# Layer norm in a four-layer decoder step: additions in place of reductions, and the variance products moved in TensorE's order

## The chip, the cores and the metric

The kernel runs on one core of a Trainium2 chip, as one program with one launch. The metric is the device time of a run in microseconds. The views come from one profiled execution of the program.

## The reference

One inference step of a decoder trunk with model width 1024 and four layers, for a prompt of 512 tokens and 8 sample tokens. Each layer has a token mixer (NSA attention, gMLP, HGRN2, NSA again) and then a SwiGLU FFN, and behind each of the eight stands a layer norm:

```python
def layer_norm(x, g, b):
    xf = x.astype(jnp.float32)
    mu = jnp.mean(xf, axis=-1, keepdims=True)
    var = jnp.mean(jnp.square(xf - mu), axis=-1, keepdims=True)
    return (xf - mu) * lax.rsqrt(var + LN_EPS) * g + b

def deepnorm(x, h, g, b):
    return layer_norm(DEEPNORM_ALPHA * x + h, g, b)
```

A ninth layer norm stands inside the gMLP mixer, on its gate values v. All of it is in float32.

## The kernel before

**Layout.** Activations lie transposed: features on the 128 partitions in eight blocks, the 520 tokens along the free axis. All work on tokens is done in two halves, columns 0 to 255 and 256 to 519. The norm takes two feature blocks at a time as one piece, so a half has four pieces j = 0 to 3, each 128 x 512 (first half) or 128 x 528 (second half).

**Products.** `mm` (L238 on) makes one output block of one half: for each k of 7 or 8 input blocks three products, high weight with high activation (L249), low weight with high activation (L250), high weight with low activation (L251). `Weights.need` at the start of an `mm` converts the weights of a unit ahead: two casts on ScalarE for the high parts (L101), two subtractions for the low parts (L102, mostly VectorE). Weight loads are issued on SP's queue, further ahead.

**Order.** The program is written out by hand: each engine's queue holds its instructions in the order in which Python emits them, and an engine works its queue in that order. Side work is written as generators. `mm` calls `tick()` after every second k, and each tick advances every generator in the list `par` by one `yield`. A tick is thus a place in TensorE's order, not a time. When an `mm` asks for activations of a half whose generator is not done, the rest of it is emitted at once (`Split.get`).

**The norm.** `ln` (L264) is such a generator, spawned when the last output block of a half has been added to x, and the sum over blocks (`add_sum`, L361 and L363, on GpSimd, the last on VectorE) is complete. In order:

- three waits (WM), then the product of the sums with a matrix of 1/1024 (L278), which gives the mean on all partitions;
- per piece a subtraction of the mean on VectorE (L285) and a square on ScalarE (L286), two pieces per tick; the squares of two pieces lie in one buffer;
- two reductions on VectorE (L294), each over the four blocks of one buffer, one per tick;
- WV = 0 waits, then two products with the same matrix (L299), accumulated: the variance;
- in the next tick the guess of the inverse root on ScalarE (`guess`: a table load at L333 if needed, logarithm L340, exponential L342); in the next one Newton step on VectorE (L349 to L353);
- per piece, one per tick: a multiply on VectorE (L307), then for each of its two blocks gain and bias on ScalarE into the high part (L312) and on GpSimd into x in place (L316); the low part, x minus high part, follows on VectorE (L272) one tick later.

There are 18 norm halves. In the second half of the last norm (`direct`) the eight blocks of squares go to the products without a reduction.

**What stands beside it.** A first half's norm runs beside the second half of the same output projection: seven blocks of four ticks, eight in the first NSA layer, or seven of three ticks (21 products) behind an FFN. A second half's norm runs beside the next stage, which computes its first blocks for the first half only: three hidden units of an FFN (two `mm` of four ticks each), or six blocks elsewhere; so in either case 24 ticks, and then TensorE needs the second half. The next stage's evictions stand among the norm's instructions: in an FFN after each eight ticks a SiLU on ScalarE (L419, with its own table, L333), a multiply on VectorE (L420), a cast on ScalarE (L210) and a subtraction on VectorE (L211); in gMLP a GELU after each four ticks, in HGRN2 a copy or a sigmoid, in NSA a copy or a sigmoid. The projections' evictions are L382 and L384 on VectorE. In gMLP the norm of v is followed by transposes (L479), copied on ScalarE (L482).

Of the kernel before, what the change touches and what calls it, by code (L numbers as in the profile page):

```python
# [11 lines left out]
OP = mybir.AluOpType  # L12
AX = mybir.AxisListType
# [7 lines left out]
CH = (8, 7, 7)  # L21
NFF = sum(CH)
SLOTS = 38
WM, WV = 3, 0


HORD, HF, HW, BUILD, SW0, SWAIT, HRATE, EARLY = (0, 1, 2, 3), 6, 1, 3, 0, 8, 2, 6
# [27 lines left out]
def wait(n):  # L55
    for _ in range(n):
        yield
# [60 lines left out]
class Split:  # L118
# [6 lines left out]
    def pair(self, j):  # L125
        if j not in self.h:
            self.h[j], self.l[j] = self.net.slot(FR), self.net.slot(FR)
        return self.h[j], self.l[j]
# [16 lines left out]
class Net:  # L145
# [118 lines left out]
    def ln(self, cols, li, sums, pair, X=None, out=None, direct=False):  # L264


        nc = self.nc
        late = []

        def rest():  # L270
            l, x, h = late.pop(0)
            nc.vector.tensor_sub(l, x, h.bitcast(FT))  # L272

        c0, c1 = cols
        n = c1 - c0
        yield from wait(WM)
        pm = self.ps()
        nc.tensor.matmul(pm[:, :n], self.ones, sums[:, :n], start=True, stop=True)  # L278
        yield
        q, sq = [], []  # L280
        for j in range(4):
            xs = pair(j, c0, c1)
            if j % 2 == 0:
                sq.append(self.flat()[:, :4 * n].rearrange("p (b t) -> p b t", b=4))
            nc.vector.tensor_sub(xs, xs, pm[:, None, :n].to_broadcast([128, 2, n]))  # L285
            nc.scalar.activation(sq[-1][:, 2 * (j % 2):2 * (j % 2) + 2], xs, AF.Square)  # L286
            if j % 2:
                yield
        for j in range(2):
            if direct:  # L290
                q += [sq[j][:, i] for i in range(4)]
            else:
                q.append(self.row()[:, :n])
                nc.vector.tensor_reduce(q[-1], sq[j].rearrange("p b t -> p t b"), op=OP.add, axis=AX.X)  # L294
            yield
        yield from wait(WV)
        pv = self.ps()
        for i, r in enumerate(q):
            nc.tensor.matmul(pv[:, :n], self.ones, r, start=i == 0, stop=i == len(q) - 1)  # L299
        y = self.row()[:, :n]  # L300
        yield
        self.guess([y], [pv[:, :n]])
        yield
        self.newton([y], [pv[:, :n]])
        for j in range(4):
            xs = pair(j, c0, c1)
            nc.vector.tensor_mul(xs, xs, y[:, None, :].to_broadcast([128, 2, n]))  # L307
            hl = X.pair(j) if X is not None else None
            for k in (0, 1):
                g, b = (t[:, li, 2 * j + k:2 * j + k + 1] for t in (self.gn, self.gb[:, :, 1]))  # L310
                if X is not None:
                    nc.scalar.activation(hl[0][:, k, c0:c1], xs[:, k], AF.Identity, scale=g, bias=b)  # L312
                if X is None and k == 0:
                    nc.scalar.activation(xs[:, k], xs[:, k], AF.Identity, scale=g, bias=b)
                else:
                    nc.gpsimd.tensor_scalar(xs[:, k], xs[:, k], g, b, op0=OP.mult, op1=OP.add)  # L316
            if X is not None:
                late.append((hl[1][:, :, c0:c1], xs, hl[0][:, :, c0:c1]))
            elif out is not None:
                out(j, c0, c1, xs)  # L320
            if len(late) > 1:
                rest()
            yield
        while late:
            rest()
            yield
# [1075 lines left out]
```

## Time and profile before

| | us |
|---|---|
| median of three runs | 3082.68 |
| lowest and highest | 3077.68, 3083.25 |
| the profiled execution | 3078.4 |
| its span, first to last instruction | 3076.7 |

The mean granted TensorE clock is 0.976 of full speed. In the rows below PE is TensorE, DVE VectorE, ACT ScalarE and POOL GpSimd. A line of the timeline gives start and duration in us, engine, source line, operation, output and input tile, shapes, the number of instructions merged into it, and in brackets how long the engine had been idle before and what released it. One matrix product in float32 stands there as two instructions.

### The profile page before, as it was taken

To read this page: it belongs to the slowest core of one execution; us is meant where nothing else is said; L and a number is where in the kernel's file an instruction comes from. 1 tells how busy PE (TensorE), PEld (TensorE's weight loads), DVE (VectorE), ACT (ScalarE), POOL (GpSimd) and SP (SyncE) were. 2 spreads that over 40 slices of the span, in tenths; PEclk is the share of its full clock that TensorE was granted. 3 is DMA by queue.
4 is the path that set the end of the run, shared out by engine and by line. 5 is a ranking of instruction groups with operands and counts; after the bars stand their busy time and mean duration, and the time that the engine had idled before them with its cause. 6 is when DMAs were issued, how large, how long until landed. Compare 5 with 4: busy or idle time off the path is not lost. (4 is left out here: it accounts for less than half of the span.)

```text
span 3076.7 us, 56298 instructions
## 1 busy us (share of the span) xinstructions
PE 2886.1 (94%) x22730; PEld 2759.4 (90%) x22730; DVE 1725.9 (56%) x3821; ACT 1293.8 (42%) x2902; POOL 473.4 (15%) x446
## 2 busy tenths in 40 slices
PE   8889889999989999999999999999988998899997
PEld 8888569999989899998899889999888876799997
DVE  4888655333566633337677773333668876533334
ACT  4666534222355432234445543122456665432322
POOL 0222141000031200004222230000312222400002
PEclk9999999999999999999999999999999999999999
DMA  5212532223223222322222223223222244233221
GB/s 173 69 59 80 165 124 90 96 77 108 71 83 97 76 90 92 101 89 71 78 71 73 76 100 94 94 80 95 81 87 63 63 155 130 97 97 94 85 86 40
DMA packets 136039, 280.61 MB, mean 91 GB/s; under 512 B 13026, under 2 KB 76002, under 8 KB 135778
## 3 DMA queue, kind: packets, MB, share of 16 engines
q1 hardware_dynamic: 127168, 261.86, 26.8%
q10 hardware_dynamic: 7458, 10.95, 1.0%
q0 software_dynamic: 1152, 4.19, 0.5%
q8 instruction: 179, 2.93, 0.4%
q14 instruction: 82, 0.67, 0.1%
HBM read 263.69 MB, written 13.27 MB: 90 GB/s over the span
## 5 line engine op out<-in xcount | busy, mean ns | idle before, releaser
L249 PE MATMUL ps<-g 128*128 128x256 f32 (+1 forms) x6176 | 1784.8, 289 | 19.5 <-ACT g L101 12.9
L250 PE MATMUL ps<-g 128*128 128x256 f32 (+1 forms) x6176 | 1758.0, 285 | 10.9 <-DVE g L102 5.8
L251 PE MATMUL ps<-g 128*128 128x256 f32 (+1 forms) x6176 | 1759.1, 285 | 3.0 <-DVE g L211 1.7
L249 PEld LDWEIGHTS ps<-g 128*128 128x128 f32 x6176 | 1180.2, 191 | 34.6 <-ACT g L101 13.3
L250 PEld LDWEIGHTS ps<-g 128*128 128x128 f32 x6176 | 1179.7, 191 | 18.3 <-DVE g L102 7.1
L251 PEld LDWEIGHTS ps<-g 128*128 128x128 f32 x6176 | 1177.5, 191 | 4.6 <-DVE g L211 2.6
L102 DVE TENSOR_TENSOR g<-g 128x512 fp32r<-128x512 f32 (+1 forms) x708 | 467.6, 711 | 59.9 <-ACT g L101 52.5
L101 ACT CAST g<-g 128x512 fp32r<-128x512 f32 (+1 forms) x788 | 426.6, 608 | 105.4 <-DVE g L102 98.1
L420 DVE TENSOR_TENSOR row<-row,ps 128x256 f32<-128x256 f32 (+1 forms) x176 | 74.8, 425 | 515.8 <-PE ps L251 515.8
L210 ACT CAST g<-row 128x256 fp32r<-128x256 f32 (+1 forms) x192 | 78.6, 410 | 503.4 <-DVE row L420 491.7
L361 POOL TENSOR_TENSOR row<-x 128x256 f32<-128x256 f32 (+1 forms) x16 | 13.3, 834 | 1452.1 <-DVE x L384 1003.1
L419 ACT ACTIVATE row<-ps 128x256 f32<-128x256 f32 (+1 forms) x176 | 67.6, 384 | 334.3 <-PE ps L251 334.1
L952 ACT ACTIVATE g<-g,nst 128x128 f32<-128x128 f32 (+3 forms) x256 | 143.0, 559 | 128.0 <-DVE nst L950 123.9
L999 PE MATMUL ps<-g 128*128 128x512 f32 x384 | 142.1, 452 | 1.2 <-DVE g L987 0.9
L964 POOL TENSOR_SCALAR g<-g,nst 128x128 f32<-128x128 f32 (+3 forms) x64 | 76.4, 1193 | 414.8 <-DVE nst L957 345.4
L950 DVE CUSTOM_DVE_ANT_0 g<-ps,ncst 128x128 f32<-128x128 f32 (+3 forms) x256 | 119.3, 485 | 37.2 <-PE ps L948 27.8
L382 DVE SCALAR_TENSOR_TENSOR x<-x,ps 128x256 f32<-128x256 f32 (+1 forms) x128 | 52.9, 422 | 153.3 <-PE ps L251 153.1
L948 PE MATMUL ps<-g 128*128 128x256 f32 (+2 forms) x512 | 124.2, 346 | 13.9 <-DVE kcS L830 5.4
L102 POOL TENSOR_TENSOR g<-g 128x512 fp32r<-128x512 f32 x80 | 105.7, 1342 | 162.4 <-ACT g L101 147.6
L384 DVE TENSOR_TENSOR x<-x,ps 128x256 f32<-128x256 f32 (+1 forms) x128 | 53.8, 424 | 135.7 <-PE ps L251 135.6
L211 DVE TENSOR_TENSOR g<-row,g 128x256 fp32r<-128x256 f32 (+1 forms) x192 | 81.7, 429 | 83.8 <-ACT g L210 83.8
L316 POOL TENSOR_SCALAR x<-x,lngn,lngb 128x256 f32<-128x256 f32 (+1 forms) x120 | 104.8, 886 | 144.7 <-ACT g L312 129.9
(239 smaller groups left out, 2842.2 us busy)
## 6 DMA issues: line engine op xcount, KB each, us to landing
g<-ffn_in SPq DMA_DIRECT2D x176, 512.0 KB, 3.6
g<-ffn_out SPq DMA_DIRECT2D x64, 448.0 KB, 3.3
g<-nsa_in SPq DMA_DIRECT2D x42, 512.0 KB, 3.8
cm<-cache_cmp SPq DMA_DIRECT2D x64, 256.0 KB, 3.6
g<-cache_slc SPq DMA_DIRECT2D x128, 128.0 KB, 2.7
g<-cache_win SPq DMA_DIRECT2D x32, 512.0 KB, 5.4
g<-ffn_out SPq DMA_DIRECT2D x32, 512.0 KB, 3.5
g<-hgrn_in SPq DMA_DIRECT2D x32, 512.0 KB, 4.0
```

The costliest lines, as they stand in the source:

```text
L101: self.nc.scalar.copy(h[:, a:b], r[:, a:b])
L102: (self.sub[a > 0] or self.nc.vector).tensor_sub(l[:, a:b], r[:, a:b], h[:, a:b].bitcast(FT))
L210: self.nc.scalar.copy(h, src)
L211: self.nc.vector.tensor_sub(l, src, h.bitcast(FT))
L249: nc.tensor.matmul(p[:, :n], H[:, s], a, start=k == 0, stop=False)
L250: nc.tensor.matmul(p[:, :n], L[:, s], a, start=False, stop=False)
L251: nc.tensor.matmul(p[:, :n], H[:, s], b, start=False, stop=k == nk - 1)
L316: nc.gpsimd.tensor_scalar(xs[:, k], xs[:, k], g, b, op0=OP.mult, op1=OP.add)
L948: nc.tensor.matmul(p[:, :nn], q, kt[:, s, :nn], start=s == 0, stop=s == 1)
L950: nc.vector.tensor_tensor_reduce(P, p[:, :n], tri[:, 512 - n:], 1.0, 3e38, OP.add, OP.min, st[:, i:i + 1])
L952: defer(lambda P=P, i=i: (self.table(LN_EXP), nc.scalar.activation(P, P, AF.Exp, bias=st[:, i:i + 1], scale=-1.0, accum_out=st[:, 4 + i:5 ...
L999: nc.tensor.matmul(o, v, PT[:, s, :512], start=start and s == 0, stop=stop and s == 1)
```

## The change

The constant WV goes from 0 to 5, and in the halves that are not direct the two reductions become three additions in place: in each buffer of squares the last two blocks are added to the first two, and then the second buffer's two to the first's. The two variance products read the two blocks that remain. Each of the first two additions is emitted behind the `yield` that follows its buffer's squares, so the first stands ahead of the subtractions of pieces two and three. The two `yield`s of the reductions stay in the direct half and are gone in the others; the five waits are in the others alone.

```diff
-WM, WV = 3, 0
+WM, WV = 3, 5
...
             nc.scalar.activation(sq[-1][:, 2 * (j % 2):2 * (j % 2) + 2], xs, AF.Square)
             if j % 2:
                 yield
-        for j in range(2):
-            if direct:
-                q += [sq[j][:, i] for i in range(4)]
-            else:
-                q.append(self.row()[:, :n])
-                nc.vector.tensor_reduce(q[-1], sq[j].rearrange("p b t -> p t b"), op=OP.add, axis=AX.X)
-            yield
-        yield from wait(WV)
+                if not direct:
+                    nc.vector.tensor_add(sq[-1][:, :2], sq[-1][:, :2], sq[-1][:, 2:])
+        if direct:
+            for t in sq:
+                q += [t[:, i] for i in range(4)]
+                yield
+        else:
+            nc.vector.tensor_add(sq[0][:, :2], sq[0][:, :2], sq[1][:, :2])
+            q = [sq[0][:, i] for i in range(2)]
+            yield from wait(WV)
         pv = self.ps()
```

## Rows read from the trace of the kernel before

**Rows 1.** The page, engines' busy time, share of the span, instructions.
```profile
PE 2886.1 (94%) x22730; PEld 2759.4 (90%) x22730; DVE 1725.9 (56%) x3821; ACT 1293.8 (42%) x2902; POOL 473.4 (15%) x446
```

**Rows 2.** Whom TensorE waited for: us in total, times, longest.
```profile
PE ps L299 <- DVE row L294: 44.6, 34, 4.1
...
PE ps L278 <- DVE row L363: 4.0, 3, 1.4
...
PE ps L251 <- DVE g L272: 1.2, 2, 0.7
```

**Rows 3.** The reductions' line: ns min/median/max, first and last start.
```profile
L294 DVE TENSOR_REDUCE row<-g x34: 1876/1942/2022, 446.8 to 3043.8; 128x256 f32<-128x1024 f32 x18, 128x264 f32<-128x1056 f32 x16
```

**Rows 4.** VectorE in order of time, a second half: start us, us.
```profile
1818.44 2.54 DVE L285 TENSOR_TENSOR x<-x,ps 128x528 f32<-128x528 f32 x4
...
1824.63 0.41 DVE L420 TENSOR_TENSOR row<-row,ps 128x256 f32<-128x256 f32 x1
...
1830.20 1.33 DVE L307 TENSOR_TENSOR x<-x,row 128x528 f32<-128x528 f32 x2
...
1833.59 1.41 DVE L102 TENSOR_TENSOR g<-g 128x512 fp32r<-128x512 f32 x2
1834.93 0.69 DVE L307 TENSOR_TENSOR x<-x,row 128x528 f32<-128x528 f32 x1
...
1839.85 0.71 DVE L272 TENSOR_TENSOR g<-x,g 128x528 fp32r<-128x528 f32 x1 [0.94 <-POOL x L316]
...
1841.88 2.50 DVE L102 TENSOR_TENSOR g<-g 128x512 fp32r<-128x512 f32 x4
```

**Rows 5.** ScalarE in the same stretch.
```profile
1819.17 2.49 ACT L286 ACTIVATE g<-x 128x528 f32<-128x528 f32 x4 [6.45 <-DVE x L285]
1821.68 1.28 ACT L333 ACT_TABLE_LOAD   x1
...
1827.83 0.48 ACT L340 ACTIVATE row<-ps,eps 128x264 f32<-128x264 f32 x1
...
1832.96 1.12 ACT L101 CAST g<-g 128x512 fp32r<-128x512 f32 x2
...
1838.42 1.28 ACT L333 ACT_TABLE_LOAD   x1
```

**Rows 6.** TensorE in the same stretch, the products at the norm.
```profile
1822.91 0.71 PE L299 MATMUL ps<-row,ones 128*128 128x264 f32 x2 [1.58 <-DVE row L294]
1824.76 0.71 PE L299 MATMUL ps<-row,ones 128*128 128x264 f32 x2 [1.14 <-DVE row L294]
...
1840.61 0.39 PE L251 MATMUL ps<-g 128*128 128x264 f32 x1 [0.59 <-DVE g L272]
```

**Rows 7.** Window, length, busy us (instructions) of PE, PEld, DVE, ACT, POOL, clock; second: L249 alone.
```profile
1825.00:1829.00 4.00, 4.00 (x21) 3.94 (x21) 1.96 (x5) 3.63 (x6) 0.00 (x0) 0.57 0.43 131
...
1829.00:1836.10 7.10, 5.64 (x21) 3.80 (x21) 1.00 0.01 2
```

**Rows 8.** The last layer's first half: products, and VectorE's last eviction.
```profile
3043.90 0.70 PE L299 MATMUL ps<-row,ones 128*128 128x256 f32 x2 [0.78 <-DVE row L294]
3045.73 0.48 PE L299 MATMUL ps<-row,ones 128*128 128x256 f32 x1 [1.14 <-DVE row L294]
...
3057.06 0.43 DVE L384 TENSOR_TENSOR x<-x,ps 128x264 f32<-128x264 f32 x1 [2.13 <-PE ps L251]
```

**Rows 9.** Sums behind a first half on GpSimd; a last eviction elsewhere.
```profile
1813.23 2.42 POOL L363 TENSOR_TENSOR row<-row,x 128x264 f32<-128x264 f32 x3 [1.21 <-DVE x L382]
...
468.09 0.43 DVE L382 SCALAR_TENSOR_TENSOR x<-x,ps 128x264 f32<-128x264 f32 x1 [2.48 <-PE ps L251]
```

**Rows 10.** TensorE at the entry of the second NSA layer.
```profile
2232.52 0.39 PE L249 MATMUL ps<-g 128*128 128x256 f32 x1 [1.66 <-ACT g L101]
2234.58 0.39 PE L250 MATMUL ps<-g 128*128 128x256 f32 x1 [1.67 <-DVE g L102]
```

**Rows 11.** ScalarE, gMLP: first transposed copy.
```profile
942.15 0.59 ACT L482 COPY g<-ps 128x512 f32<-128x512 f32 x1 [0.68 <-PE ps L479]
```


## Prediction

> **What bounds the kernel now.** I read the busy shares first: TensorE works 94% of the span, VectorE 56%, ScalarE 42% [rows 1]. So time is won or lost only where TensorE stands still, and the second view is who TensorE waited for [rows 2]. The largest entry by far is this change's place: the variance products (L299) waited 34 times for the reductions (L294), 44.6 us in all. There are 17 norm halves with reductions (18 halves, one is direct), two reductions each; a reduction takes 1.94 us [rows 3]. Two small entries matter as much: the mean product waited 4.0 us for the last sum (L278 on L363), and products of the next stage waited 1.2 us, twice, for the normed activations' low halves (L251 on L272) [rows 2]. The latter says that the norm of a second half, as it stands, ends just when TensorE needs it. Third I read one second half, at the entry of an FFN, queue by queue [rows 4 to 6]; that pattern occurs four times.
>
> **What the change edits.** A tick is six products of a projection, two of them of line L249; 21 of L249 in 7.10 us [rows 7] make it 0.7 us. Counted from the norm's spawn, the mean product stands in tick 4 in both. Before, the variance products stand in tick 9, the guess in 10, the four scalings in 11 to 14, the last low half in 15. After, the two yields of the reductions go and five waits come: products in 12, guess in 13, scalings in 14 to 17, last low half in 18. Net it is three ticks, not five. The direct half has no wait and loses nothing. Costed at nothing: the squares' two slots, of 38, stay taken five ticks longer, and two row buffers fewer are used; the moved steps issue DMAs only for gMLP's v and the first half of the final output, on SP, where the weights for the next products are already loaded (with that cover gone, a first output store of the last layer would come 2 us later, still ahead of the second half's).
>
> **VectorE.** Two reductions (3.88 us) become three additions of two 256-column blocks. No such addition is in the trace; the in-place multiply of the same shape takes 0.69 [rows 4], so 2.1 us; bounds 1.2 (the 0.41 of a multiply half as wide, L420 [rows 4]) and 2.9 (half a reduction each [rows 3]). But they are not freely placed. The first stands in VectorE's order behind the first two subtractions and ahead of the other two, and needs their squares, so that everything queued behind it on VectorE waits too. With S the start of the first subtraction, a subtraction every 0.61 and lasting 0.70 (four in 2.54 [rows 4]) and a square about 0.64 (four in 2.49 [rows 5]): second square ends S+2.0, first addition, subtractions from S+2.65, last square S+4.6, two additions, products ready at S+6.1. Before, the second product started at 1824.76 with S = 1818.44 [rows 4, 6]: S+6.32. VectorE saves 1.8 us of work and the chain 0.2.
>
> [...]
>
> **First halves.** Their two waits are 0.78 + 1.14 us [rows 8], nine times much the same. Three ticks later TensorE arrives about when the additions end: some 0.3 is left, so TensorE gets 1.6 to 2.1 us ahead. The tail (guess, scaling, low halves) does not start earlier; it starts 0.3 later, as both products now run after the wait. The second half's S follows that tail on VectorE and GpSimd: after the last low half come three sums on GpSimd, 2.42 us [rows 9], then the sum on VectorE, then S. With the tail three ticks later in the order one sum stands ahead of it, 0.8 less. So S comes 0.5 us earlier where this chain leads, and the full 1.9 where VectorE waited 2.48 for TensorE at the last eviction [rows 9].
>
> **Second halves into an FFN (four).** Before, S to the logarithm L340 is 9.39 us, 2.37 on to the first scaling, and 10.36 on to the end of the last low half, 1840.56 [rows 4, 5]: 22.1 in all. TensorE was waiting for it, 0.59 us [rows 6]. After:
> - ScalarE: last square S+4.6 instead of S+3.2, sigmoid-linear table load 1.28, activation, VectorE's multiply and the cast to about S+7.1. A cast pair of the next weights (1.12, at 1832.96 before [rows 5]) is issued before tick 13 and now stands ahead of the guess: two pairs to S+9.4, table load 1.28, logarithm at S+10.7 instead of S+9.4. Plus 1.3.
> - The scalings: before, all four pieces come ahead of the FFN's second eviction (its table load is at 1838.42 [rows 5]). After, that eviction falls in tick 16, between piece three and piece four. From its table load to the second of the four subtractions at 1841.88 it takes 4.7 us [rows 4, 5]; about 0.4 of that is VectorE's own queue, so 4.3. Without the cast pair in between, piece three's scaling starts 3.3 after the first (before 4.73, less the 1.41 of the two subtractions at 1833.59), its ScalarE part ends at 5.1, the eviction and casts end at 9.4, and piece four needs 3.3 more: 12.7 instead of 10.36. Plus 2.3.
> The chain is 3.6 longer (bounds: 1.3, if VectorE's part of the eviction does not hold piece four, and 4.5). S comes 0.5 earlier in the shown one: it ends 3.1 us later, and TensorE, with its wait at the products cut, simply waits in front of piece three instead (about 4.6 us, row of type L251 on L272). In two of four S comes 1.9 earlier and TensorE had about 0.4 to spare: +1.3 each. The fourth lies between: +2.2. Sum +7.9.
>
> **The other places.** Into gMLP and HGRN2 an eviction already stood amid the pieces, so it only changes place; the cast pair and the later squares cost the same 1.3, S comes 0.6 earlier, and up to 2 us were to spare: +0.8 and +1.7 (bounds 0 and +6 together). Into the second NSA layer TensorE stood 1.66 us for a cast and as much for its low half [rows 10], a cast behind the norm's pieces on ScalarE; it comes some 2 to 3 us earlier: -3 (bounds -5, 0). gMLP's own norm: the second half's guess falls behind a GELU eviction with its table load and a cast pair, and the first transposed copy (942.15 [rows 11]) stands behind the pieces on ScalarE; I get it at 946 to 947: +4 (bounds -5, +6: the wait before its products was the second longest, and if the copy isn't late all of that comes back). Last layer: the first half's gain stays, since VectorE waits 2.13 for TensorE at the last eviction [rows 8]: -2.
>
> [...]
>
> [...]
>
> **Sum.** 7.9 + 2.5 - 3 + 4 - 2 + 7 = +16 us. The profiled execution took 3078.4 (span 3076.7), 4.3 under the median of 3082.7 of the runs shown, so it becomes about 3094 there and **3098 us** by the median.
>
> **Rivals.**
> - *The tail fits.* If the second halves' pieces are ready without a wait, the 44.6 us [rows 2] shrink to about 5 and the slow stretches go at some places: -45, 3037 us. For it: it is the largest wait. Against: it decides at the low halves, where TensorE already waited and has at most 2 us to spare. 12%.
> - *VectorE's saved time lies on the path.* 17 x 1.8 = 31 us: 3051. For it: evictions queue behind reductions (L420 at 1824.63 [rows 4]). Against: squares pace the additions. 8%. [...]
> - *The change of order is a wash.* The FFN eviction does not hold piece four, the chain grows only by 1.3 and S comes as much earlier: 3081, between 3072 and 3090. 20%.
> - *Forecast:* 60%, its own range 3088 to 3114.
>
> About 0.2%, 6 us, is what a measurement can tell from no change. Slower: 60% and 3 of the wash, 63%. Same: 13 of the wash. Faster: 4 of the wash, 12 and 8, 24%. The range goes from 3046, which leaves out most of the first rival, to 3114.
>
> **What would show it.** L299's wait falls from 44.6 to about 20 us, all in one wait per half; L251 on L272 rises from 1.2 to 30 or more; L278 on L363 rises from 4 to about 10; VectorE's busy time falls by about 31. At the FFN entries a table load and activation stand between the third and fourth pair of L312. I am wrong if L251 on L272 stays under 10 us: then the first rival holds, or if the first additions do not wait for squares.

## The result, and the profile after

The changed kernel takes 3101.72 us, the median of four runs (3100.41 to 3102.89), against 3080.35 for the kernel before in the same comparison: a ratio of 1.0069, 95% interval 1.0052 to 1.0087, so 21 us slower. The profiled execution took 3100.9, its span 3099.2, 22.5 more than before. In the changed kernel the lines behind the norm's squares have moved by two: the variance products are L301, the additions L290 and L296, logarithm L342, scaling multiply L309, its ScalarE part L314, table load L335, the FFN's eviction L421 and L422.

First the page's busy shares of after, then whom TensorE waited for, as in [rows 1] and [rows 2]:

```profile
PE 2891.2 (93%) x22730; PEld 2767.5 (89%) x22730; DVE 1703.1 (55%) x3838; ACT 1295.3 (42%) x2902; POOL 462.1 (15%) x446
```

```profile
PE ps L251 <- DVE g L272: 38.7, 24, 4.6
PE ps L301 <- DVE g L296: 16.1, 13, 3.7
...
PE ps L494 <- ACT g L484: 4.7, 1, 4.7
PE ps L278 <- DVE row L365: 4.0, 6, 1.2
```

The wait at the products fell from 44.6 to 16.1, and 28.5 us were freed. The wait for low halves rose from 1.2 to 38.7, which takes 37.5 back. Of the rest the largest parts are TensorE's own busy time, 5.1 us longer for the same 22730 instructions, and a new wait of 4.7 at gMLP's transposed copies (L494). VectorE did 22.8 us less work, and the kernel took longer all the same.

Where it happens is seen from the mean products (L278), one per half and at the same place in both programs: the time from one to the next, after less before, is the gain or loss of that stretch. Over the nine first halves (mean product of the first half to that of the second) it sums to -14.4 us; over the eight stretches behind second halves to +37.0, of which the four FFN entries have 22.9. (The stretch ahead of the first mean product, which holds the loads at the start and varies by up to 6 us between kernels that don't differ in it, is left out here and below, and so is the one behind the last, which varies by up to 1.7.)

This is the second half of [rows 4 to 6], at the same FFN entry, in after; VectorE first (columns as there). S, the start of the first subtraction, is 1836.19:

```profile
1836.19 1.31 DVE L285 TENSOR_TENSOR x<-x,ps 128x528 f32<-128x528 f32 x2
1838.22 0.71 DVE L290 TENSOR_TENSOR g<-g 128x528 f32<-128x528 f32 x1 [0.71 <-ACT g L286]
1838.84 1.31 DVE L285 TENSOR_TENSOR x<-x,ps 128x528 f32<-128x528 f32 x2
1840.86 0.71 DVE L290 TENSOR_TENSOR g<-g 128x528 f32<-128x528 f32 x1 [0.71 <-ACT g L286]
1841.61 0.71 DVE L296 TENSOR_TENSOR g<-g 128x528 f32<-128x528 f32 x1
...
1852.44 0.99 DVE L309 TENSOR_TENSOR x<-x,row 128x528 f32<-128x528 f32 x1
...
1856.31 0.42 DVE L422 TENSOR_TENSOR row<-row,ps 128x256 f32<-128x256 f32 x1 [1.69 <-ACT row L421]
...
1858.93 0.70 DVE L309 TENSOR_TENSOR x<-x,row 128x528 f32<-128x528 f32 x1
...
1861.59 0.71 DVE L272 TENSOR_TENSOR g<-x,g 128x528 fp32r<-128x528 f32 x1 [1.34 <-POOL x L318]
```

ScalarE in the same stretch:

```profile
1843.33 2.18 ACT L101 CAST g<-g 128x512 fp32r<-128x512 f32 x4
1845.52 1.28 ACT L335 ACT_TABLE_LOAD   x1
1846.82 0.48 ACT L342 ACTIVATE row<-ps,eps 128x264 f32<-128x264 f32 x1
...
1853.47 1.11 ACT L314 ACTIVATE g<-x,lngb,lngn 128x264 fp32r<-128x264 f32 x2 [1.42 <-DVE x L309]
1854.60 1.28 ACT L335 ACT_TABLE_LOAD   x1
1855.89 0.39 ACT L421 ACTIVATE row<-ps 128x256 f32<-128x256 f32 x1
...
1857.07 1.14 ACT L101 CAST g<-g 128x512 fp32r<-128x512 f32 x2
1859.67 1.11 ACT L314 ACTIVATE g<-x,lngb,lngn 128x264 fp32r<-128x264 f32 x2 [1.46 <-DVE x L309]
```

TensorE there, the products and the first wait for the third piece:

```profile
1842.37 1.16 PE L301 MATMUL ps<-g,ones 128*128 128x264 f32 x4 [2.09 <-DVE g L296]
...
1860.31 0.59 PE L251 MATMUL ps<-g 128*128 128x264 f32 x1 [4.64 <-DVE g L272]
```

Read it in this order. The additions wait for the squares twice, 0.71 us each, and the second pair of subtractions stands behind the first wait. The products start at S+6.2, the logarithm at S+10.6. ScalarE finishes the third piece's high parts at 1854.6 and then takes the FFN's table, eviction and casts before it touches the fourth (1859.67). The fourth multiply on VectorE stands meanwhile behind the eviction's multiply and the weights' subtractions, and the last low half ends at 1862.30, S+26.1, where it was S+22.1. TensorE stands 4.64 us in front of the third piece.

The granted clock of TensorE behind its two waits there (windows: length, busy us, instructions, clock, DMA share, GB/s), in after:

```profile
1842.30:1846.30 4.00, 3.93 (x19) 0.67 0.40 122
...
1860.30:1864.30 4.00, 3.63 (x15) 0.52 0.31 123
```

and in the kernel before, behind its wait of 0.59 for the last low half ([rows 6]):

```profile
1840.60:1844.60 4.00, 3.99 (x33) 1.00 0.43 131
```

There the granted clock was 1.00; behind the 4.64 us wait it is 0.52.

### The profile page after: what moved, and what is told of

Same layout as the page of the kernel before. It is cut to its first block, busy times and chain, and to the rows that moved or that the text cites. A ratio compares the mean times of both kernels' runs of the same rounds, so it can differ in the third digit from the quotient of the medians.

```text
span 3099.2 us, 56311 instructions
## 1 busy us (share of the span) xinstructions
PE 2891.2 (93%) x22730; PEld 2767.5 (89%) x22730; DVE 1703.1 (55%) x3838; ACT 1295.3 (42%) x2902; POOL 462.1 (15%) x446
## 5 line engine op out<-in xcount | busy, mean ns | idle before, releaser
L249 PE MATMUL ps<-g 128*128 128x256 f32 (+1 forms) x6176 | 1787.5, 289 | 22.4 <-ACT g L101 15.7
L251 PE MATMUL ps<-g 128*128 128x256 f32 (+1 forms) x6176 | 1766.5, 286 | 40.8 <-DVE g L272 38.7
L251 PEld LDWEIGHTS ps<-g 128*128 128x128 f32 x6176 | 1181.8, 191 | 47.5 <-DVE g L272 44.6
L249 PEld LDWEIGHTS ps<-g 128*128 128x128 f32 x6176 | 1184.1, 192 | 36.5 <-ACT g L101 16.1
L250 PEld LDWEIGHTS ps<-g 128*128 128x128 f32 x6176 | 1183.5, 192 | 15.7 <-POOL g L102 6.0
L422 DVE TENSOR_TENSOR row<-row,ps 128x256 f32<-128x256 f32 (+1 forms) x176 | 74.9, 425 | 537.5 <-PE ps L251 529.7
L363 POOL TENSOR_TENSOR row<-x 128x256 f32<-128x256 f32 (+1 forms) x16 | 13.0, 814 | 1456.3 <-DVE x L386 1006.3
L421 ACT ACTIVATE row<-ps 128x256 f32<-128x256 f32 (+1 forms) x176 | 67.8, 385 | 338.3 <-PE ps L251 338.2
L386 DVE TENSOR_TENSOR x<-x,ps 128x256 f32<-128x256 f32 (+1 forms) x128 | 54.0, 424 | 133.1 <-PE ps L251 133.0
L950 PEld LDWEIGHTS ps<-g 128*128 128x128 f32 x512 | 85.7, 200 | 40.0 <-DVE nst L952 12.6
```

The source lines that it names most:

```text
L249: nc.tensor.matmul(p[:, :n], H[:, s], a, start=k == 0, stop=False)
L250: nc.tensor.matmul(p[:, :n], L[:, s], a, start=False, stop=False)
L251: nc.tensor.matmul(p[:, :n], H[:, s], b, start=False, stop=k == nk - 1)
L950: nc.tensor.matmul(p[:, :nn], q, kt[:, s, :nn], start=s == 0, stop=s == 1)
```

## The experiments

Two values measured at the FFN entries carry the comparison: S to the start of the logarithm, and S to the end of the last low half (median of the four entries; they agree within 0.3 us). "First" and "second" are the sums of steps described above, against the profile of the kernel before. The last columns are the waits at the variance products and at low halves, and the ratio to the kernel before with its 95% interval. Source lines behind the norm move by up to three more from kernel to kernel.

| kernel | log | last low | first | second | products | low halves | ratio |
|---|---|---|---|---|---|---|---|
| before | 9.4 | 22.1 | 0 | 0 | 44.6 | 1.2 | 1 |
| changed | 10.6 | 26.1 | -14.4 | +37.0 | 16.1 | 38.7 | 1.0069 [1.0052, 1.0087] |
| adds_t9 | 9.6 | 22.3 | +9.9 | -1.4 | 55.2 | 2.5 | 1.0032 [1.0020, 1.0043] |
| adds_t10 | 9.6 | 23.1 | -4.9 | +23.2 | 45.6 | 13.3 | 1.0033 [1.0020, 1.0045] |
| adds_t11 | 9.6 | 25.9 | -8.7 | +38.8 | 29.8 | 34.7 | 1.0083 [1.0067, 1.0100] |
| reduce_t12 | 10.6 | 26.0 | -15.6 | +31.3 | 13.3 | 38.4 | 1.0056 [1.0039, 1.0073] |
| reduce_split | 9.4 | 22.1 | -15.6 | +4.5 | 29.6 | 7.7 | 0.9968 [0.9955, 0.9980] |
| split_5_2 | 9.6 | 22.3 | -14.5 | +7.9 | 35.0 | 7.3 | 0.9981 [0.9972, 0.9990] |
| guess_first | 9.6 | 26.7 | -14.6 | +42.4 | 18.4 | 42.5 | 1.0090 [1.0076, 1.0103] |
| pieces_together | 10.6 | 22.3 | -14.4 | +17.3 | 18.2 | 18.9 | 0.9993 [0.9982, 1.0003] |
| late_fourth | 9.4 | 26.0 | -0.3 | +27.3 | 45.5 | 18.1 | 1.0096 [1.0081, 1.0111] |
| adds_behind | 8.2 | 20.9 | -18.2 | +1.2 | 21.5 | 8.5 | 0.9935 [0.9922, 0.9948] |
| adds_behind_together | 8.2 | 20.9 | -18.2 | +1.2 | 24.0 | 8.8 | 0.9942 [0.9930, 0.9954] |
| behind_late | 9.2 | 24.6 | -18.2 | +29.3 | 6.6 | 40.7 | 1.0030 [1.0020, 1.0040] |

**The parts of the change by themselves, and how late is late.** Three kernels keep the additions and shorten the five waits to two (the products where they stood), three and four; the fourth keeps the reductions and moves the products as far as the change does.

```diff
-WM, WV = 3, 5
+WM, WV = 3, 2    # adds_t9;  3 in adds_t10, 4 in adds_t11
```

```diff
# reduce_t12, against the kernel before
-WM, WV = 3, 0
+WM, WV = 3, 3
```

> The three additions, but two waits instead of five, so that the variance products stand in tick 9 as before. Order theory (the loss is the norm's tail, moved three ticks back past the next stage's eviction and casts): no loss, the products are ready 0.2 us earlier per half, so 2 us under before, between 8 under and 2 over; TensorE waits for the products again (over 35 us) and for low halves under 5 us. Rival (the additions themselves cost, because VectorE stands for the squares in front of the second pair of subtractions): 10 us or more over before.

> The additions with three waits: products in tick 10, last low half in tick 16, still ahead of an FFN's second eviction. Order theory: no loss, 6 us under before (14 under to 1 over), because the chain of a second half is as long as before and first halves put TensorE a little ahead. Rival (each tick later costs alike, a third of 21 us): 7 us over before.

> The additions with four waits: products in tick 11, fourth piece in tick 16, its low half in 17, behind an FFN's second eviction. Order theory: the loss comes in this step, 10 to 20 us over before, with low halves waited for 20 us or more. Rival (each tick alike): 14 us over before, so that this run only counts beside the one a tick earlier.

> The kernel before with its two reductions and three waits: products in tick 12 as in the changed kernel. Order theory: the whole loss is there without any addition, 20 to 27 us over before, low halves waited for 35 us or more. Rival (the additions cost): 3 us over before at most.

Medians 3088.69, 3089.60, 3104.65 and 3095.09, beside 3078.61. From three to four waits the time jumps by 15 us, and the low-half wait with it, from 13.3 to 34.7: that is the step in which the last low half falls behind the FFN's eviction, and the second halves lose 15.6 us more, all of it at the four FFN entries (9.4 become 25.7). reduce_t12 shows that the order alone makes most of the loss, +16.5 of 21, with nearly the same second-half chain. All four missed their numbers, adds_t11 by 6 over and reduce_t12 by 3.5 under; and adds_t9 and adds_t10, expected under before, are 10 and 11 us over, adds_t9 as its rival had it. Additions at the old place cost 10 us, all in first halves (+9.9): five of the nine lose 1.7 to 1.8 each, and the wait at the products is 10.6 longer in all, 5.0 of it in first halves. adds_t10 loses elsewhere: its first halves gain 4.9, and of the 23.2 in second halves 8.2 lie at the entry of the second NSA layer, which was not tried apart. VectorE in the last layer's first half of adds_t9, beside [rows 8]:

```profile
3044.55 0.69 DVE L290 TENSOR_TENSOR g<-g 128x512 f32<-128x512 f32 x1 [0.70 <-ACT g L286]
3045.16 1.28 DVE L285 TENSOR_TENSOR x<-x,ps 128x512 f32<-128x512 f32 x2
3046.36 0.42 DVE L386 TENSOR_TENSOR x<-x,ps 128x264 f32<-128x264 f32 x1
3047.13 1.07 DVE L290 TENSOR_TENSOR g<-g 128x512 f32<-128x512 f32 x1 [0.36 <-ACT g L286]
3048.24 0.69 DVE L296 TENSOR_TENSOR g<-g 128x512 f32<-128x512 f32 x1
```

and TensorE:

```profile
3048.99 1.89 PE L301 MATMUL ps<-g,ones 128*128 128x256 f32 x4 [2.46 <-DVE g L296]
```

Where the first product stood between two waits of 0.78 and 1.14, one wait of 2.46 now stands ahead of both, and the two take 1.89 behind it, where each took 0.70. An eviction (L386) has slipped in ahead of the second addition too, which still waits 0.36 for its square behind it. The logarithm starts 8.3 behind the first subtraction (3050.91 less 3042.57); it was 7.3. This half and the one before it are the worst; in the other seven the logarithm is only 0.3 later, TensorE waits 2.4 to 2.5 in one piece where it had waited 1.9 to 2.0 in two, and what makes up the rest of the 1.7 to 1.8 was not tried apart. So the first halves want the products late, whatever sums the squares.

**Late in first halves only.** If the gain is in the first and the loss in the second halves, they can be parted.

```diff
# split_5_2, against the changed kernel
-            yield from wait(WV)
+            yield from wait(WV if c1 < T else 2)
# reduce_split, against the kernel before
-        yield from wait(WV)
+        yield from wait(3 if c1 < T else 0)
```

> The kernel before with its reductions, and three waits ahead of the variance products in first halves only (second halves stay at their place). Theory (order: a later place lets TensorE get ahead at first halves, and costs only at second halves, where the tail comes too late for the next stage): the steps at the first halves stay as with the reductions all moved, about -15 us, and the second halves give back at most what S does not follow, 0 to 1.5 each; 5 to 12 us under before, ratio 0.996 to 0.9985, the wait of the variance products about 28 us, that of L251 on L272 under 10. Rival (what first halves gain is waited out again at the second halves, whose chain does not start earlier): within 2 us of before, and L251 on L272 or the second halves' L299 grow by what the first lose.

> The changed kernel, with the five waits in first halves only and two in second halves, so that these stand where they stood before. Theory (order): the first halves keep their -14 us, the second halves lose the +37 they cost in the changed kernel but for 0 to 1.5 each: 3 to 12 us under before, some 30 under the changed kernel. Rival (the additions themselves cost, as they did at the earliest place, about 9 us whatever the order): at before or up to 6 over it.

Medians 3067.74 and 3072.04, beside 3078.17: both under before. The first halves keep their -15, and what comes back in the second halves is 4 to 8 us, as the order theory said for both. By the medians the additions are 4 us behind the reductions in this order, though they take less of VectorE; the intervals overlap a little.

**Which step holds the second halves up.** Three edits each move one thing.

```diff
# guess_first, against the changed kernel (second halves that are not direct)
         y = self.row()[:, :n]
-        yield
+        if c1 < T or direct:
+            yield
         self.guess([y], [pv[:, :n]])
         yield
+        if c1 == T and not direct:
+            yield
```

```diff
# pieces_together, against the changed kernel
             if len(late) > 1:
                 rest()
-            yield
+            if c1 < T or X is None or j < 2:
+                yield
+            elif j == 3:
+                rest()
```

```diff
# late_fourth, against the kernel before
         for j in range(4):
+            if j == 3 and c1 == T and X is not None:
+                yield from wait(3)
             xs = pair(j, c0, c1)
```

> The changed kernel, with the guess of second halves emitted right behind the products, in their step, so that the cast pair of the next weights stands behind it on ScalarE; the scalings keep their place. Theory (the cast pair costs 1.1 us of chain at each second half): S to logarithm 9.4 to 9.6 instead of 10.6 at the FFN entries, 5 to 9 us under the changed kernel, so 13 to 17 over before. Rival (only the place of the last pieces counts): within 2 us of the changed kernel, about 21 over before.

> The changed kernel, with the third and fourth piece of second halves, and their low parts, emitted in one step, so that all four pieces stand ahead of the next stage's second eviction (the norm inside gMLP is left as it is). Theory (the eviction between pieces three and four costs 2.3 us at each FFN entry, some less elsewhere): 9 to 15 us under the changed kernel, 7 to 13 over before; L251 on L272 falls from 38.7 to 20 to 28. Rival (the chain is late from its start, by the products' late place and the cast pair, and the eviction then pays what the pieces save): within 3 us of the changed kernel.

> The kernel before, reductions and products at their place, with one edit: in second halves the fourth piece is emitted three steps later, so that at an FFN entry the second eviction stands between pieces three and four, as in the changed kernel. Theory (that one eviction, with its table load and casts, makes the second halves' loss): at an FFN entry the last low half ends some 4 us later than before (S+26 instead of S+22.1), L251 on L272 rises from 1.2 to 25 to 40 us, and the kernel takes 18 to 32 us longer than before. Rival (the late products and the late guess make the loss, the eviction only fills time that the chain loses anyway): under 8 us over before.

Medians 3106.33, 3076.01 (beside 3078.17) and 3105.21 (beside 3076.45). ScalarE of pieces_together at the same FFN entry:

```profile
1830.85 1.11 ACT L314 ACTIVATE g<-x,lngb,lngn 128x264 fp32r<-128x264 f32 x2 [1.41 <-DVE x L309]
1832.65 1.11 ACT L314 ACTIVATE g<-x,lngb,lngn 128x264 fp32r<-128x264 f32 x2 [0.69 <-DVE x L309]
1833.78 1.28 ACT L338 ACT_TABLE_LOAD   x1
```

and of late_fourth:

```profile
1856.18 1.11 ACT L314 ACTIVATE g<-x,lngb,lngn 128x264 fp32r<-128x264 f32 x2 [1.56 <-DVE x L309]
1857.31 1.28 ACT L335 ACT_TABLE_LOAD   x1
...
1862.38 1.10 ACT L314 ACTIVATE g<-x,lngb,lngn 128x264 fp32r<-128x264 f32 x2 [1.46 <-DVE x L309]
```

With the fourth piece ahead of the table load the last low half ends at S+22.3, with the late logarithm and all; with it behind, in a kernel that is otherwise the one before, at S+26.0. The eviction between pieces three and four is worth 3.8 and 3.9 us of chain at an FFN entry in the two directions (26.1 less 22.3, 26.0 less 22.1). The kernels differ by 23 (by the ratios) and 29 us, of which the stretches at the four FFN entries have 16.3 and 25.6; the rest lies at other entries, where the same edits also move pieces. pieces_together gained more than I had expected (9 to 15), late_fourth lost what the theory said, though its wait for low halves stayed under the expected 25 (18.1): it keeps the wait at the products too, so TensorE comes later to the low halves, and the clock is low behind both waits (0.63 and 0.50, below).

The cast pair is a different matter. In guess_first the logarithm does move ahead of it, to S+9.6, but the kernel is not 5 to 9 us under the changed one: it is 5 over by the medians and 6 by the ratios, whose intervals overlap. ScalarE, then VectorE:

```profile
1847.58 0.42 ACT L347 ACTIVATE row<-row 128x264 f32<-128x264 f32 x1
1847.91 1.13 ACT L101 CAST g<-g 128x512 fp32r<-128x512 f32 x2
```

```profile
1848.55 1.30 DVE L102 TENSOR_TENSOR g<-g 128x512 fp32r<-128x512 f32 x2 [1.99 <-ACT g L101]
1849.76 0.43 DVE L354 SCALAR_TENSOR_TENSOR row<-ps,row 128x264 f32<-128x264 f32 x1
```

The root's guess is ready at 1848.0, but the Newton step stands on VectorE behind the pair's subtractions, which wait for the casts: it starts at S+12.3 (S = 1837.48) instead of S+11.6 in the changed kernel. The pair is paid in either place.

**The place of the first addition.** In split_5_2 and in the changed kernel the first addition holds two subtractions. Two kernels emit all three additions behind the fourth subtraction, with five and two waits; one of them also has pieces three and four of second halves in one tick (the edit of pieces_together). The last kernel has five waits in all halves.

```diff
# adds_behind, against split_5_2; behind_late: the same edit against the changed kernel
-                if not direct:
-                    nc.vector.tensor_add(sq[-1][:, :2], sq[-1][:, :2], sq[-1][:, 2:])
...
         else:
+            for t in sq:
+                nc.vector.tensor_add(t[:, :2], t[:, :2], t[:, 2:])
             nc.vector.tensor_add(sq[0][:, :2], sq[0][:, :2], sq[1][:, :2])
```

> Three additions with five waits in first and two in second halves, as in the split kernel, but all three additions are emitted behind the fourth subtraction, none between the second and third. Theory (the interleaved first addition holds up the subtractions and so the squares: products ready at S+6.1): now four subtractions end at S+2.5, the squares at S+3.2, the additions at S+4.6 to 4.9; the wait of L301 in second halves falls by 1.2 to 1.5 each, in all from 35 to 22 to 26 us; the second half's tail is not earlier, since the logarithm stands behind the eviction and casts on ScalarE (9.4 behind S), so that part of it comes back at L251 on L272: 2 to 10 us under the split kernel, 8 to 17 under before. Rival (the squares' place makes no difference): within 2 us of the split kernel, L301 still about 35.

> The same, and the third and fourth piece of second halves emitted in one step, with their low parts. Theory (the order of the pieces against cast pairs and evictions still costs a little at the entries of gMLP, HGRN2 and NSA): the rest of L251 on L272 (about 7 us) falls under 3; 0 to 6 us under the kernel without this edit. Rival (no eviction is left between the pieces that counts): within 2 us of it, either way.

> The changed kernel, products at their late place in all halves, with the one edit that the first two additions stand behind the fourth subtraction. Theory (two losses add up in the changed kernel's second halves: the interleaved addition, worth 1.2 of chain as the last comparison showed, and the eviction between the pieces, some 4): logarithm 1.0 to 1.4 earlier behind S at the FFN entries, 9.2 to 9.6, the last low half at S+24.7 to 25.1, and 6 to 14 us under the changed kernel, 8 to 16 over before; L251 on L272 falls from 38.7 to 27 to 33. Rival (the eviction between the pieces begins at its own time and sets the end alone): the last low half still at S+26, within 3 us of the changed kernel.

Medians 3057.08 and 3057.30 beside 3076.45, and 3085.38 beside 3077.06. VectorE in adds_behind at the same FFN entry, S = 1807.92:

```profile
1807.92 2.54 DVE L285 TENSOR_TENSOR x<-x,ps 128x528 f32<-128x528 f32 x4
1810.38 1.50 DVE L295 TENSOR_TENSOR g<-g 128x528 f32<-128x528 f32 x2
1811.91 0.71 DVE L296 TENSOR_TENSOR g<-g 128x528 f32<-128x528 f32 x1
...
1828.08 0.71 DVE L272 TENSOR_TENSOR g<-x,g 128x528 fp32r<-128x528 f32 x1 [0.93 <-POOL x L318]
```

and ScalarE:

```profile
1816.09 0.48 ACT L342 ACTIVATE row<-ps,eps 128x264 f32<-128x264 f32 x1
```

No subtraction or addition waits there any more, the sums are ready at S+4.7 instead of S+6.1, and the chain ends at S+20.9. I had expected the tail to stay where ScalarE holds it, at 9.4 behind S; it came to 8.2, since the first eviction moves up with it, and the gain over split_5_2 was 14 us (ratios 0.9981 and 0.9935) where I had put 2 to 10. behind_late is 12 us under the changed kernel by the ratios, as expected; its wait for low halves did not fall (40.7), because TensorE also gets past the products 1.4 earlier. The same eviction is worth 3.8 here too (24.63 less 20.87). Pieces in one tick add nothing where the eviction already stands behind them, and low halves still wait 8.8: there the rival held. adds_behind is the fastest kernel of the series, 0.65% under before.

## Why the prediction came out right

The forecast was 3098 us, measured 3101.72, and the path was the one described: freed at the products, lost in front of the third piece. That the number is so near is in part luck: +16 was forecast and +21.4 measured between the medians, and 2.3 of that gap does not show in 3098, because the kernel before was faster in the comparison (3080.35) than in the runs that the forecast started from (3082.68). By its steps:

- *Products, logarithm, chain.* Predicted S+6.1, S+10.7 and 25.7 for the chain; measured S+6.2, S+10.6 and 26.1. The queue orders worked out by hand from [rows 4, 5] held to 0.4 us. Of the 3.6, I put 1.3 at the guess (measured 1.2) and 2.3 at the pieces (measured 2.7 in the shown entry). The runs say how to read these two: the 1.3 and the 1.41 that I took off piece three are one cast pair that changes sides, and they cancel (pieces_together ends at 22.3 with the late guess, before 22.1). What remains is the eviction, 2.3 + 1.41 = 3.7 by my working, 3.8 by the runs. It is nearly all of the 4.0 that the chain grew by at the FFNs.
- *First halves.* At the four FFN entries S was to come 0.5 earlier in the shown one, 1.9 in two, and between these in the fourth; measured from one S to the next it comes 0.6, 1.9, 1.9 and 1.6 earlier. Counted by the mean products, as in the sums above, the gain is 0.5 to 0.6 behind the first three FFNs and 1.6 to 3.2 at the other places.
- *FFN entries.* +7.9 and about 4 of the 7 estimated for the clock, 11.9 in all, net of the first halves ahead of them; measured +14.4.
- *gMLP and HGRN2 entries.* The most mis-sized term: +2.5 and 2 of the same 7, measured +4.5 and +4.4. "An eviction already stood amid the pieces, so it only changes place" fails: their logarithms came 1.2 and 2.6 later behind S, the chains grew by 1.6 and 4.3, and into gMLP S itself came 0.35 later, not 0.6 earlier; with two pieces in one tick the chains are back at 20.4 and 21.9, before 22.4 and 20.5. Here too the two pieces' order against the eviction was the larger part, which I had left out.
- *Second NSA layer, gMLP's own norm, last layer.* -3, +4, -2; measured -1.6, +3.2, -2.3. The new wait of gMLP's copies is the 4.7 of L494.
- *The clock.* The +7 of the sum was an estimate, 1 us at each of seven entries, and no run shows it. What the runs show in its place: TensorE's busy time grew by 5.1 for the same 22730 instructions, with a mean granted clock of 0.974 in the profiled execution where it was 0.976, and in the windows above the clock was 0.52 behind a wait of 4.64 where it had been 1.00 behind one of 0.59; no run takes this apart from the waits.
- *L278 on L363* was to rise from 4 to 10 and stayed at 4.0. TensorE meets another wait first: the next stage's products for the first half need its low parts, which now come later in the order. Three times, behind an FFN, it waits about 1.7 there, ahead of the mean product. The place in after:

```profile
1438.71 0.39 PE L251 MATMUL ps<-g 128*128 128x256 f32 x1 [1.01 <-DVE g L272]
...
1440.32 0.39 PE L251 MATMUL ps<-g 128*128 128x256 f32 x1 [0.64 <-DVE g L272]
...
1442.02 1.25 PE L278 MATMUL ps<-row,ones 128*128 128x264 f32 x2 [0.92 <-DVE row L365]
```

- *VectorE's busy time* was to fall by 31 and fell by 22.8. The lines of the scaling multiply and the additions in after (busy us, mean ns, idle before), beside 64.5 us for the reductions:

```profile
L309 DVE TENSOR_TENSOR x<-x,row 128x512 f32<-128x512 f32 (+1 forms) x64 | 46.2, 746 | 0.6
...
L290 DVE TENSOR_TENSOR g<-g 128x512 f32<-128x512 f32 (+1 forms) x34 | 25.4, 746 | 21.4 <-ACT g L286 21.3
...
L296 DVE TENSOR_TENSOR g<-g 128x512 f32<-128x512 f32 (+1 forms) x17 | 12.6, 739 | 0.6
```

The additions take 38.0, so 26.5 is saved, not 31; the scaling multiplies took 3.3 more (their mean was 694 ns): eleven of them took 0.96 to 0.99, as at 1852.44.

- *The rival that VectorE's saved time lies on the path* was turned down because the squares pace the additions. They do so only as the additions are placed: behind the four subtractions, 12 to 14 us come out of it. There the additions gain over reductions in the same order (adds_behind 0.9935, reduce_split 0.9968), and at the place that the changed kernel gives them they do not (1.0069, reduce_t12 1.0056). *That the tail fits* fell with the 38.7 us in front of low halves; the slow stretches that it counts on are such as the one at a clock of 0.57 in [rows 7]. *The wash* asked that the eviction not hold piece four; late_fourth shows that it does.

What stays open: why the gMLP norm's own second half loses 2 to 6 us in each kernel whose first halves are as late as in the changed one was not tried apart, and the 4 us between split_5_2 and reduce_split are argued from the interleaved addition, not isolated at that place.

## What to carry to other kernels

A wait that ends on the busiest engine is not the price of what it waits for. Ask which later instruction of the same chain that engine meets next, and write the queues of the other engines between the two by hand, because one foreign eviction with its table load, standing between two pieces, cost nearly as much here as all the freed waits were worth. Give parts with slack and parts without their own place in the order: the same move won 14 us in first halves and lost 37 in second ones. And where an in-place sum replaces a reduction, put it behind the work that feeds its own inputs, since in a queue kept in order an early start holds up what stands behind it: here the sums were ready at S+6.1 with the first addition ahead of the third subtraction, and at S+4.7 with all three behind the fourth.

## What the runs showed of the hardware

- The same 22730 TensorE instructions took 2872.9 us of busy time in adds_behind_together and 2899.9 in late_fourth, 27 us apart; the mean granted clock was 0.981 and 0.972. late_fourth waits at two places at each FFN entry, and at the entry shown above the clock is low behind both (0.63 in the first of these windows, 0.50 in the second); in adds_behind the same stretch, behind a wait of 2.78 at the products, stayed at 1.00.

```profile
1847.00:1850.00 3.00, 3.00 (x19) 0.63 0.27 102
1863.00:1867.00 4.00, 3.63 (x15) 0.50 0.31 123
```

```profile
1812.68 1.16 PE L301 MATMUL ps<-g,ones 128*128 128x264 f32 x4 [2.78 <-DVE g L296]
...
1812.60:1816.60 4.00, 3.92 (x29) 1.00 0.36 111
```

So the clock may or may not be low behind a wait of 2 to 3 us: 0.67 behind 2.09 in the changed kernel, 1.00 behind 2.78 here. What decides between these two was not tried.
- A VectorE multiply of 128x528 took 0.99 us in one place and 0.70 in another (rows at 1852.44 and 1858.93 of the changed kernel). GpSimd was at work beside all eleven slow ones, but also beside 18 that took about 0.7, so what makes them slow stays open.
